# Attention probabilities transposed in 32x32 tiles by VectorE and regrouped by two transfers, in place of TensorE, for 16 of 24 heads

## The chip, the core and the metric

The kernel runs on one core of a Trainium2 chip. The metric is the device time of one execution, in microseconds (us). The kernel before took 937.93 us (median of 3 runs, 937.87 to 938.56). A separate, profiled execution gave the trace that is read here.

The core has engines that each work through their own list of instructions strictly in order: PE (TensorE, matrix products), DVE (VectorE), ACT (ScalarE), POOL (GpSimd), and SP, which in this kernel only issues transfers (DMAs). An instruction whose input is not ready makes everything behind it on that engine wait.

## What is computed

A decoder trunk of two layers on 256 tokens of width 1024, in float32. Each layer is a half-step SwiGLU FFN, a mixer, and a second half-step FFN. Both mixers hold softmax attention with heads of 64: layer 0 has 8 heads of masked attention (three dilation patterns, which one additive mask expresses) beside a gated MLP; layer 1 has 16 heads of causal attention, since with 256 tokens there is only the own block.

```
for layer in range(DEPTH):
    h = h + 0.5 * swiglu(rms_norm(h, ffn1_norm[layer]), ...)
    hn = rms_norm(h, mix_norm[layer])
    h = h + (ab_mixer(hn, ...) if layer % 2 == 0 else c_mixer(hn, ...))
    h = h + 0.5 * swiglu(rms_norm(h, ffn2_norm[layer]), ...)
return rms_norm(h, final_norm)
# attention of one head:  p = softmax(q k^T * scale + mask);  out = p v
```

## The kernel before

**Products in three parts.** Every float32 operand is split into a high part (rounded to fp32r, by ACT) and a low part (the rest, by DVE), and a product is three matmuls, high by high, high by low, low by high (`mm3`, L265). Of the weights, each chunk of 128x2048 is loaded by SP into one of 3 `raw` buffers (L139), split by ACT (`whi`, L172) and DVE (`wlo`, L173) into one of 4 buffer pairs, and used by PE. A chunk's load waits for the split that frees its `raw` buffer.

**The mixers.** `ab_mixer` (layer 0) and `c_mixer` (layer 1) run projections tile by tile, and a table of slots (`Slots`) says behind which tile a step of the attention is issued: one slot is one tile of 24 matmuls with 256 columns (or 12 with 512). The steps of a head are these.

- `put_q`, `put_k` turn a projected tile into the q and k of a pair of heads: for k DVE multiplies by the norm (`qk`, L659), ACT writes the high part (L683), POOL or DVE the low part (L685).
- `scores(h)`: four matmuls (L700, L701); DVE adds the mask and takes the maximum for each half (L704, two instructions with their reads `nm`); ACT takes the exponentials and their sums (L707); DVE the reciprocal `rl` (L710); POOL multiplies the probabilities `pr` by it, in two instructions (L714), for all but the last heads, where DVE does.
- `turn(h)`: PE transposes the head's 128x384 probabilities in three instructions (L723) into PSUM; ACT and DVE split them into `pth` and `ptl` (`split`, L271).
- `weighted(p)`: six matmuls multiply v by the probabilities of a pair of heads; ACT and DVE split the result into the tiles `mix` (L271).

In `ab_mixer`, DVE and ACT also prepare the gated part between these: `put_v` (`vtl`, L821), `keep_g` with the normalized `vn` (L853, by way of ACT's gelu and squares, DVE's `msg` and POOL's `rsg`), `put_u` (`uT`, L882), and `mixing(g)`, for which PE multiplies `vn` (L859) and DVE adds and multiplies (`tmp`, L864 and L865).

The order on each engine is made by the scheduler of the framework from the program's own order and what is ready. The last FFN already contains a transposition of the kind that the change adds: `turn_back` (L486) turns 128x128 in 32x32 tiles by DVE (L491), sends it to a scratch in memory (L494) and fetches it regrouped (L496).

## Time and profile before

| | us |
|---|---|
| median of 3 runs | 937.93 |
| the profiled execution, as timed | 937.01 |
| its span, first to last instruction | 935.3 |
| PE busy in the span | 927.7 |
| DVE busy | 612.1 |
| ACT busy | 499.2 |
| POOL busy | 83.0 |

The profile shows, for one execution, the busy time of each engine, the chain of work that ended last (followed back from the end, at each step to what released it), groups of instructions by line, and a timeline. In a group's row stand the line, the engine, the operation, written tile <- read tiles, shape and number, then busy us and the mean ns of one, then the engine's idle time before them and what ended it. In a timeline row stand the start in us, the duration, the engine and the instruction; the bracket at its end is the idle time before it and what ended that. SPq marks what SP issues.

### The profile page before, as it was taken

What the parts mean: (1) busy time and instruction counts of PE and PEld (TensorE: products, weight loads), DVE (VectorE), ACT (ScalarE), POOL (GpSimd) and SP (SyncE); (2) the same over time, 40 slices, a digit from 0 to 9 for tenths busy, and PEclk for the clock granted to TensorE, in tenths of its full rate; (3) what the DMA queues carried; (4) which work ended last, traced back from release to release, by engine and by line L of the source; (5) the groups of instructions that cost most, each with busy time, mean ns of one, the idle gap of its engine ahead of it and who ended that gap; (6) DMA issues with size and microseconds to landing.
All of it is one profiled execution on the core that took longest, in us unless ns stands there. A gap on an engine that the chain in (4) does not pass through costs nothing.

```text
span 935.3 us, 18101 instructions
## 1 busy us (share of the span) xinstructions
PE 927.7 (99%) x7655; PEld 907.4 (97%) x7655; DVE 612.1 (65%) x892; ACT 499.2 (53%) x782; POOL 83.0 (9%) x114
## 2 busy tenths in 40 slices
PE   9999999999999999999999999999999999999997
PEld 9999999999999999999999999999999999999886
DVE  7866556676888666555756665567787786656543
ACT  7744444468667454444454544456786665445431
POOL 0000000034210000000000000002574000000000
PEclk9999999999999999999999999999999999999999
DMA  8755554665336555555555555556543377555521
GB/s 320 281 212 181 189 194 162 223 222 180 136 136 226 188 211 188 183 175 206 204 184 200 204 180 170 203 184 220 177 139 136 137 243 269 186 188 210 190 90 46
DMA packets 28305, 176.99 MB, mean 189 GB/s; under 512 B 3264, under 2 KB 4672, under 8 KB 9152
## 3 DMA queue, kind: packets, MB, share of 16 engines
q1 hardware_dynamic: 26928, 173.65, 52.5%
q10 hardware_dynamic: 1296, 2.18, 0.7%
q8 instruction: 60, 0.98, 0.4%
q14 instruction: 21, 0.17, 0.0%
HBM read 173.72 MB, written 2.10 MB: 188 GB/s over the span
## 4 chain that ended last, share of the span: by engine, by line
PE 98%; issue 1%; DMA 0%; ACT 0%; SPq 0%; DVE 0%; POOLq 0%; POOL 0%
PE bank L266 30%; PE bank L267 30%; PE bank L268 30%; PE bank L567 2%; PE bank L571 2%; PE bank L568 2%; PE bank L723 1%; PE bank L700 1%; PE bank L701 1%; DMA x<-in_x 0%; PE bank L343 0%; PE bank L859 0%; PE bank L361 0%; PE bank L455 0%; PE bank L456 0%
## 5 line engine op out<-in xcount | busy, mean ns | idle before, releaser
L172 ACT ACTIVATE whi<-raw 128x1024 fp32r<-128x1024 f32 (+3 forms) x352 | 330.5, 985 | 350.1 <-issue 282.9
L173 DVE TENSOR_TENSOR wlo<-raw,whi 128x1024 fp32r<-128x1024 f32 (+3 forms) x352 | 389.6, 1141 | 126.7 <-ACT whi L172 125.8
L266 PE MATMUL bank<-xTh,whi 128*128 128x256 f32 x1616 | 447.9, 277 | 0.0
L267 PE MATMUL bank<-xTl,whi 128*128 128x256 f32 x1616 | 446.7, 276 | 0.0
L268 PE MATMUL bank<-xTh,wlo 128*128 128x256 f32 x1616 | 446.6, 276 | 0.0
L267 PEld LDWEIGHTS bank<-xTl,whi 128*128 128x128 f32 x1616 | 303.5, 188 | 0.2
L266 PEld LDWEIGHTS bank<-xTh,whi 128*128 128x128 f32 x1616 | 303.5, 188 | 0.0
L268 PEld LDWEIGHTS bank<-xTh,wlo 128*128 128x128 f32 x1616 | 303.5, 188 | 0.0
L267 PE MATMUL bank<-hTl,whi 128*128 128x256 f32 x528 | 145.8, 276 | 0.0
L266 PE MATMUL bank<-hTh,whi 128*128 128x256 f32 x528 | 145.8, 276 | 0.0
L268 PE MATMUL bank<-hTh,wlo 128*128 128x256 f32 x528 | 145.8, 276 | 0.0
L266 PEld LDWEIGHTS bank<-hTh,whi 128*128 128x128 f32 x528 | 99.1, 188 | 0.0
L268 PEld LDWEIGHTS bank<-hTh,wlo 128*128 128x128 f32 x528 | 99.1, 188 | 0.0
L267 PEld LDWEIGHTS bank<-hTl,whi 128*128 128x128 f32 x528 | 99.1, 188 | 0.0
L506 DVE TENSOR_TENSOR hm<-gs,bank 128x512 f32<-128x512 f32 x44 | 30.1, 687 | 77.7 <-PE bank L268 77.3
L503 DVE TENSOR_TENSOR gs<-bank,row 128x512 f32<-128x512 f32 x44 | 30.0, 689 | 47.8 <-PE bank L268 47.8
L266 PE MATMUL bank<-mixh,whi 128*128 128x256 f32 x128 | 35.3, 281 | 0.0
L267 PE MATMUL bank<-mixl,whi 128*128 128x256 f32 x128 | 35.1, 277 | 0.0
L268 PE MATMUL bank<-mixh,wlo 128*128 128x256 f32 x128 | 35.0, 277 | 0.0
L714 POOL TENSOR_SCALAR pr<-pr,rl 128x128 f32<-128x128 f32 (+1 forms) x36 | 30.8, 870 | 25.2 <-DVE rl L710 14.1
L653 POOL MEMSET ql<- 64x256 f32 x12 | 3.7, 307 | 328.7 <-ACT whi L172 170.3
L567 PE MATMUL bank<-whi,hTh 128*128 128x512 f32 x80 | 31.1, 389 | 0.0
(134 smaller groups left out, 877.4 us busy)
## 6 DMA issues: line engine op xcount, KB each, us to landing
raw<-in_weights SPq DMA_DIRECT2D x149, 1024.0 KB, 4.9
raw<-in_weights SPq DMA_DIRECT2D x12, 768.0 KB, 4.4
raw<-in_weights SPq DMA_DIRECT2D x6, 512.0 KB, 6.5
x<-in_x SPq DMA_DIRECT2D x4, 264.0 KB, 4.0
raw<-in_weights SPq DMA_DIRECT2D x4, 256.0 KB, 4.3
away<-xn SPq DMA_DIRECT2D x2, 512.0 KB, 5.5
xr<-away SPq DMA_DIRECT2D x8, 128.0 KB, 5.7
fg<-in_final_norm ACTq DMA_DIRECT2D x1, 512.0 KB, 3.7
```

What stands on the lines that cost most here:

```text
L172: nc.scalar.activation(hi, r, AF.Copy)
L173: nc.vector.tensor_sub(lo, r, hi.bitcast(F32))
L266: nc.tensor.matmul(p, sh, mh, start=start, stop=False)
L267: nc.tensor.matmul(p, sh, ml, start=False, stop=False)
L268: nc.tensor.matmul(p, sl, mh, start=False, stop=stop)
L503: nc.vector.tensor_mul(g, both(pg), twice(norm["row"]))
L506: nc.vector.tensor_mul(hm, g, both(pu))
L567: nc.tensor.matmul(banks[t, h], sh, w[0][kw][:, cs], start=k == 0, stop=False)
L568: nc.tensor.matmul(banks[t, h], sh, w[1][kw][:, cs], start=False, stop=False)
L571: nc.tensor.matmul(banks[t, h], sl, w[0][kw][:, cs], start=False, stop=k == FT - 1)
L700: nc.tensor.matmul(sc[:, b * S : (b + 1) * S], q[:, bs], k, start=True, stop=False)
L714: share = engine.tensor_scalar(pr[:, cs], pr[:, cs], rl[:, b : b + 1], None, op0=ALU.mult)
```

## The change

For the heads below `nheads - 4` (4 of 8 in layer 0, 12 of 16 in layer 1) the transposes by PE and the split out of PSUM are gone. In their place:

- Once POOL has scaled a head's `pr`, DVE transposes its 32x32 tiles into a tile `turned` that four heads share (L722 of the changed kernel, a `StreamTranspose` of 128x12x32). Four heads form a group.
- Behind the fourth head, `send` issues 12 transfers from SP's queue to a scratch in memory, each 32 partitions with 4x128 elements (runs of 512 bytes).
- Some slots later, `fetch` issues two transfers that read the scratch back, regrouped, one for each pair of heads, each 128 partitions with 12 runs of 64 elements (256 bytes).
- Some slots later again, `part` splits what was fetched: ACT copies (128x768) into `pth` and DVE subtracts into `ptl`, both placed behind the last split of weights (`issue_after`).

`weighted` for these heads stands 4 to 7 slots later than before, and in layer 1 the scores of heads 4 to 11 one or more slots earlier. The last four heads of each layer keep the transposes by PE. The buffers `pr` and `qk` become fewer, a gap tile becomes smaller, and the order of elements in `pth` and `ptl` changes, so that a product's moving operand is contiguous.

In the built program of the changed kernel 24 transposes are left on PE of 72; all other matmuls stay. DVE's list gets 16 `StreamTranspose` and loses 16 of the 128x384 subtractions for 8 of 128x768; on SP's queue the 12 transfers of a group, one or two loads of weights, and the two transfers of `fetch` follow each other.

```diff
@@ -34,7 +34,7 @@
 LINE, SHIFT = 64, 16
-EDGE, GAP = 56, 240
+EDGE, GAP = 56, 112

@@ -169,8 +169,7 @@
                 hi, lo = (t.rearrange("p (k c) -> p k c", k=reset) for t in (hi, lo))
-            nc.scalar.activation(hi, r, AF.Copy)
-            nc.vector.tensor_sub(lo, r, hi.bitcast(F32))
+            self.last = nc.scalar.activation(hi, r, AF.Copy), nc.vector.tensor_sub(lo, r, hi.bitcast(F32))

@@ -644,8 +643,9 @@

-        qs, ks, probs, pts = {}, {}, {}, {}
-        pairs, flying = (4, 5) if rows else (2, 4)
+        qs, ks, probs, pts, sent = {}, {}, {}, {}, {}
+        pairs = 4 if rows else 2
+        late = nheads - 4
         seconds = [mp.tile([128, 2 * S + LINE], F32R, name=f"ql{i}") for i in range(pairs)]
@@ -655,7 +655,7 @@
         def scaled(bk):
-            t = mp.tile([128, S], F32, name="qk", bufs=3)
+            t = mp.tile([128, S], F32, name="qk", bufs=2)
             nc.vector.tensor_mul(t, bk[:, :S], norm["row"])
@@ -692,7 +692,13 @@
             sc = bank()
-            pr = mp.tile([128, 384], F32, name="pr", bufs=flying)
+            if h % 4 == 0:
+                probs["turned"] = mp.tile([128, 3, 4, 4, 32], F32, name="turned")
+            turned = probs["turned"]
+            if h < late:
+                pr = mp.tile([128, 384], F32, name="pr", bufs=3)
+            else:
+                pr = turned.rearrange("p m j h r -> p (m j h r)")[:, h % 4 * 384 : (h % 4 + 1) * 384]
             nm = wk.tile([128, 2], F32, name="nm")
@@ -712,8 +718,41 @@
                 share = engine.tensor_scalar(pr[:, cs], pr[:, cs], rl[:, b : b + 1], None, op0=ALU.mult)
+            if h < late:
+                nc.vector.transpose(turned[:, :, :, h % 4].rearrange("p m j r -> p (m j) r"),
+                                    pr.rearrange("p (b c) -> p b c", c=32))
+                if h % 4 == 3:
+                    send(h // 4)
             probs[h] = pr
             return power, share
+
+        def send(g):
+
+            sent[g] = dram.tile([4, 32, 3, 4, 128], F32, name=f"sent{nheads}{g}")
+            for i in range(4):
+                for m in range(3):
+                    nc.sync.dma_start(sent[g][:, :, m, i].rearrange("j c f -> c j f"),
+                                      probs["turned"][i * 32 : (i + 1) * 32, m].rearrange("c j h r -> c j (h r)"))
+
+        def fetch(g):
+
+            src = sent.pop(g).rearrange("j c m i f -> (j c) (m i) f")
+            for q in range(2):
+                pts[2 * g + q] = parts = part_tiles()
+                nc.sync.dma_start(parts[1].bitcast(F32).rearrange("p b h r -> p b (h r)"),
+                                  src[:, :, q * 64 : (q + 1) * 64])
+
+        def part(g):
+
+            with tc.issue_after(st.last[0].ins), tc.issue_after(st.last[1].ins):
+                for q in range(2):
+                    hi, lo = pts[2 * g + q]
+                    nc.scalar.activation(hi, lo.bitcast(F32), AF.Copy)
+                    nc.vector.tensor_sub(lo, lo.bitcast(F32), hi.bitcast(F32))
+
+        def part_tiles():
+
+            return [mp.tile([128, 12, 2, 32], F32R, name=n, bufs=2) for n in ("pth", "ptl")]

@@ -722,21 +761,22 @@
             if j == 0:
-                pts[p] = [mp.tile([128, 2, 384], F32R, name=n, bufs=2) for n in ("pth", "ptl")]
-            return split(pts[p][0][:, j, :], pts[p][1][:, j, :], tp[:, :384])
+                pts[p] = part_tiles()
+            return split(*(t[:, :, j] for t in pts[p]), tp[:, :384].rearrange("p (b r) -> p b r", r=32))

         def weighted(p):
-            o = bank().rearrange("p (j c) -> p j c", j=2)
-            pth, ptl = pts.pop(p)
+            o = bank()
+            parts = [t.rearrange("p b h r -> p (b h r)") for t in pts.pop(p)]
             vs = slice(p * 128, (p + 1) * 128)
-            mm3(o, v[0][:, 0, vs], v[1][:, 0, vs], pth[:, :, :256], ptl[:, :, :256], True, False)
-            mm3(o[:, :, 128:], v[0][:, 1, vs], v[1][:, 1, vs], pth[:, :, 256:], ptl[:, :, 256:], False, True)
+            mm3(o, v[0][:, 0, vs], v[1][:, 0, vs], *(t[:, :512] for t in parts), True, False)
+            mm3(o[:, 256:], v[0][:, 1, vs], v[1][:, 1, vs], *(t[:, 512:] for t in parts), False, True)
             for j in range(2):
                 r = slice(j * 64, j * 64 + 64)
-                done = split(mix[0][r, p], mix[1][r, p], o[r, j, :].rearrange("p (t c) -> p t c", t=NT))
+                done = split(*(m[r, p].rearrange("p t (i r) -> p (t i) r", r=32) for m in mix),
+                             o[r].rearrange("p (b h r) -> p b h r", h=2, r=32)[:, :, j])
             return done

-        return put_q, put_k, scores, turn, weighted
+        return put_q, put_k, scores, fetch, part, turn, weighted

@@ -827,7 +867,7 @@
             uT = mp.tile([128, 4, S], F32, name="uT")
-            put_q, put_k, scores, turn, weighted = make_attention(mp, slice(0, 384), 8, v, mix)
+            put_q, put_k, scores, fetch, part, turn, weighted = make_attention(mp, slice(0, 384), 8, v, mix)

@@ -872,10 +912,12 @@
             slots.at((21,), lambda _: st.release(tc, scores(7), True))
-            slots.at((10, 10, 12, 12, 22), turn)
+            slots.at((13,), fetch)
+            slots.at((17,), part)
+            slots.at((22,), lambda _: turn(4))
             slots.at((22,), lambda _: st.release(tc, turn(5), True))
             slots.at((23, 23), lambda i: turn(6 + i))
-            slots.at((13, 14, 24), weighted)
+            slots.at((18, 19, 24), weighted)
             slots.at((25,), lambda _: st.release(tc, weighted(3)))
@@ -896,12 +938,14 @@
             v = v_tiles(mp, D)
-            put_q, put_k, scores, turn, weighted = make_attention(mp, slice(384, 768), 16, v, mix, True)
+            put_q, put_k, scores, fetch, part, turn, weighted = make_attention(mp, slice(384, 768), 16, v, mix, True)

             slots = Slots()
-            slots.at((5, 6, 7, 8, 12, 13, 14, 15, 16, 17, 18, 19, 24, 24, 25, 25), scores)
-            slots.at((9, 9, 11, 11, 16, 16, 18, 18, 20, 20, 22, 22, 26, 26, 27, 27), turn)
-            slots.at((11, 13, 18, 20, 22, 24, 28, 29), weighted)
+            slots.at((5, 6, 7, 8, 11, 12, 13, 14, 15, 16, 17, 18, 24, 24, 25, 25), scores)
+            slots.at((14, 20, 25), part)
+            slots.at((15, 16, 21, 22, 26, 27, 28, 29), weighted)
+            slots.at((12, 17, 23), fetch)
+            slots.at((26, 26, 27, 27), lambda i: turn(12 + i))
             step = slots.step
```

## Prediction

> **What bounds the kernel now.** I read the share of each engine first, then the chain that ended last, the idle time of PE by what ended it, and then timelines around the attention.
>
> ```profile
> PE 927.7 (99%) x7655; PEld 907.4 (97%) x7655; DVE 612.1 (65%) x892; ACT 499.2 (53%) x782; POOL 83.0 (9%) x114
> PE 98%; issue 1%; DMA 0%; ACT 0%; SPq 0%; DVE 0%; POOLq 0%; POOL 0%
> ```
>
> ```profile
> PE bank L442 <- DVE warm L435: 1.1, 1, 1.1
> ```
>
> The chain is PE from end to end, and the only wait of PE that the trace lists is the one of 1.1 us at the start. So time comes off only if PE gets less to do, and every late operand is added in full. The mean shares of DVE and ACT hide how full they are beside the attention of layer 1:
>
> ```profile
> 660.00:670.00 10.00, 10.00 (x80) 9.60 (x79) 6.91 (x20) 7.42 (x19) 6.25 (x10) 1.00 0.59 202
> 680.00:690.00 10.00, 10.00 (x87) 9.87 (x86) 8.99 (x26) 7.47 (x22) 7.11 (x9) 1.00 0.49 154
> ```
>
> In this view of windows the columns behind PE and PEld are DVE, ACT and POOL: from 680 to 690 us DVE works 8.99 of 10 us, with PE at 10.00. A wait put on DVE there has hardly any idle time to go into.
>
> **What is removed.** Each row below is the transposes of two heads.
>
> ```profile
> 219.84 0.66 PE bank L723 x6
> ...
> 715.50 0.66 PE bank L723 x6
> ```
>
> They are the first and the last of the eight groups that go (16 heads); four more stay. Gain if PE never waits: 8 x 0.66 = **5.3 us**. The products with the probabilities keep their matmuls, so nothing else comes off PE.
>
> [...]
>
> **What is added on DVE.** The operation itself has a neighbour in the last FFN, and the slope with size is seen where one line runs with two widths:
>
> ```profile
> L491 DVE STREAM_TRANSPOSE xn<-x 128x128 f32<-128x128 f32 x16 | 3.6, 278 | 0.0
> L704 DVE CUSTOM_DVE_ANT_0 pr<-bank,mask 128x256 f32<-128x256 f32 x8 | 3.3, 419 | 0.0
> L704 DVE CUSTOM_DVE_ANT_0 pr<-bank,mask 128x128 f32<-128x128 f32 x8 | 2.3, 285 | 0.0
> L173 DVE TENSOR_TENSOR wlo<-raw,whi 128x768 fp32r<-128x768 f32 x26 | 23.8, 954 | 26.1 <-ACT whi L172 25.8
> L173 DVE TENSOR_TENSOR wlo<-raw,whi 128x1024 fp32r<-128x1024 f32 x272 | 324.3, 1225 | 91.5 <-ACT whi L172 91.1
> L172 ACT ACTIVATE whi<-raw 128x768 fp32r<-128x768 f32 x26 | 20.7, 839 | 39.6 <-issue 39.6
> ```
>
> A transposition of 128x384 is at least 0.28 us and at most 3 x 0.278 = 0.83. With 134 ns more for each 128 columns it is 278 + 2 x 134 = 546 ns; I take 0.55. Of the split, one instruction of 128x768 takes 0.95 on DVE and 0.84 on ACT, where a pair of 128x384 took 1.0 and 0.86 (rows below), so the work there stays as it is.
>
> The duration matters less than the wait in front of it. In the built program each transposition stands right behind its head's reciprocal `rl`, or a few instructions later, and waits for POOL's share of that head. These rows show how long that is:
>
> ```profile
> 659.56 0.16 DVE L710 RECIPROCAL rl<-l 128x2 f32<-128x2 f32 x1
> 660.29 0.74 DVE L821 SCALAR_TENSOR_TENSOR vtl<-bank,rstd,vth 128x512 fp32r<-128x512 f32 x1
> 662.83 0.35 DVE L704 CUSTOM_DVE_ANT_0 pr<-bank,mask,score 128x128 f32<-128x128 f32 x1 [1.57 <-PE bank L701]
> 668.59 0.17 DVE L710 RECIPROCAL rl<-l 128x2 f32<-128x2 f32 x1 [0.40 <-ACT pr L707]
> 669.74 1.31 DVE L173 TENSOR_TENSOR wlo<-raw,whi 128x1024 fp32r<-128x1024 f32 x1 [0.98 <-ACT whi L172]
> 671.42 1.00 DVE L271 TENSOR_TENSOR ptl<-bank,pth 128x384 fp32r<-128x384 f32 x2
> 674.17 0.42 DVE L659 TENSOR_TENSOR qk<-bank,row 128x256 f32<-128x256 f32 x1
> ```
>
> ```profile
> 659.88 3.00 POOL L714 TENSOR_SCALAR pr<-pr,rl 128x128 f32<-128x128 f32 x4 [2.58 <-DVE rl L710]
> 666.18 1.50 POOL L714 TENSOR_SCALAR pr<-pr,rl 128x128 f32<-128x128 f32 x2 [3.30 <-DVE rl L710]
> 675.13 1.54 POOL L685 TENSOR_TENSOR k<-qk,k 64x256 fp32r<-64x256 f32 x2 [2.46 <-ACT k L683]
> ```
>
> POOL starts 659.88 - 659.56 = 0.32 behind `rl` and takes 1.50 for a head's two instructions. The transposition can start 1.8 us after `rl`, and until then DVE does only what the list puts between the two: one `vtl` (0.7), one mask pair (0.285 + 0.419 = 0.7), or nothing. Everything behind it on DVE waits too: masks of the next heads, splits of weights, `qk`.
>
> **What is moved.** In layer 1 the scores of head 4 stand one slot earlier on PE, and the transposes and the product that stood before them are gone or later. PE therefore asks sooner for what DVE now brings later.
>
> ```profile
> 665.38 0.28 PE L700 MATMUL bank<-k,q 128*128 128x256 f32 x1
> ...
> 679.11 0.28 PE L700 MATMUL bank<-k,q 128*128 128x256 f32 x1
> ...
> 736.33 0.40 PE L266 MATMUL bank<-pth,vth 128*128 128x512 f32 x1
> ...
> 737.38 0.28 PE L266 MATMUL bank<-mixh,whi 128*128 128x256 f32 x1
> ```
>
> The first two rows are the scores of heads 3 and 4, 13.73 us apart: four tiles, the four score matmuls (0.46), two transposition groups (2 x 0.66) and one product of a pair (737.38 - 736.33 = 1.05). A tile is thus (13.73 - 0.46 - 1.32 - 1.05)/4 = 2.72. In the changed list three tiles and the scores are left, 8.6: PE asks **5.1 us** sooner.
>
> *Scores of head 4.* They wait for k, that is DVE's `qk`, ACT's high part, POOL's low part. In the changed list the four transpositions before `qk` stand behind 0.7, 0, 0.7 and 0 of other work, so DVE waits 1.1 + 1.7 + 1.0 + 1.7, about 5.4, and works 4 x 0.55 = 2.2. Off go the subtractions of heads 0 and 1 (1.0), and the old idle times 1.57 + 0.40 + 0.98 = 3.0 soak up as much. DVE is late by 5.4 + 2.2 - 1.0 - 3.0 = 3.6. The low part of k was ready at 675.13 + 1.54/2 = 675.9, a margin of 3.2 to 679.11. Stall: 5.1 + 3.6 - 3.2 = **5.5**.
>
> *From there to the product of heads 0 and 1.* DVE must do five mask pairs (3.5), four `rl` (0.7), the splits of two and a half chunks (five halves of 1.2, 6.1), six 64- or 128-row pieces of q and k (0.42 each, 2.5), four transpositions (2.2) and the first `ptl` (0.95): 15.9. Three of the waits add 3.3 (1.8 less 0.55, 0.7 and 0.7 of work between). PE has four tiles (10.9), five heads' scores (2.3) and five matmuls of 0.23 before the one that reads `ptl`: 14.3. Stall: 19.2 - 14.3, about **4.8**. Groups 1 and 2 follow the same list, but their waits find the slack that these two stalls have made: 0.
>
> *Layer 0, `mixing(0)`.*
>
> ```profile
> 214.23 1.22 DVE L173 TENSOR_TENSOR wlo<-raw,whi 128x1024 fp32r<-128x1024 f32 x1 [0.51 <-ACT whi L172]
> 217.50 0.17 DVE L710 RECIPROCAL rl<-l 128x2 f32<-128x2 f32 x1 [0.84 <-ACT pr L707]
> ...
> 229.71 1.01 DVE L271 TENSOR_TENSOR ptl<-bank,pth 128x384 fp32r<-128x384 f32 x2
> 233.21 1.14 DVE L853 SCALAR_TENSOR_TENSOR vn<-gv,rsg,vgain 128x128 f32<-128x128 f32 x4 [1.12 <-POOL rsg L274]
> ```
>
> ```profile
> 236.81 0.61 PE L859 MATMUL bank<-wsT,vn 128*128 128x128 f32 x4
> ```
>
> Its second matmul reads the `vn` of the second token tile, whose first quarter was ready at 233.21 + 0.35, a margin of 3.3. Two transposition groups and two products no longer stand before it, so PE asks 1.32 + 2.10 = 3.4 sooner. DVE waits 1.0 + 1.0 + 1.5 + 1.7 = 5.2 for POOL and transposes for 2.2, saves two pairs of `ptl` (2.0) and the idle 0.51 + 0.84: late by 4.05. Stall: 3.4 + 4.05 - 3.3, about **4.1**. From there to the product of heads 0 and 1 DVE's list is 10.3 and PE's 9.1, worked out in the same way: **1.2**.
>
> **The transfers** I cost at nothing, because DVE's list covers them:
>
> ```profile
> 769.58 1.64 SPq L496 DMA_DIRECT2D xr<-away  x3
> ```
>
> ```profile
> DMA to landing us min/median/max: 3.6/5.7/7.3
> ```
>
> One issue is 1.64/3 = 0.55. `rl` of head 3 stood at 668.59; three waits and transpositions before it (1.1 + 1.7 + 1.0 + 1.65), less 1.57 + 0.40 of idle time, put it at 672.1, and 1.8 + 0.55 later, at 674.5, the fourth transposition is done. Twelve issues (6.6), a landing of 3.6, two more issues (1.1) and a landing of 5.7 to 7.3 end by 693.1. DVE starts on head 4's mask at about 679.5 (674.0 + 5.5) and comes to `ptl`, 18.2 of work and waits later, at 697.7. Cover: some 5 us, less ACT's 0.84. SP's queue holds weight loads behind them, which land 9 to 14 us before they are split and have two more chunks behind that; a delay of about 10 us fits.
>
> **The sum**, on the profiled execution: 937.0 - 5.3 + 5.5 + 4.8 + 4.1 + 1.2 = 947.3. The median lies 0.9 over that execution, so **948.2**. Twelve transpositions lie in these stalls: at 0.28 each the sum falls by 3.2 (945), at 0.83 it grows by 3.4 (952). POOL's shares, 1.5 here, took up to 2.4 where DVE worked beside them, which adds up to 3. Own range 942 to 954.
>
> **Rivals.**
> *PE stays dense.* The scheduler's list is strict, but if DVE's waits fall into idle time that I counted as needed, only the 5.3 is seen: 932.6. For it: DVE has 35% idle over the span. Against: both windows above.
> *DVE is on time, the transfers decide.* Then the last transposition of a group is done at 668.59 + 1.8 + 0.55 = 671, the fetch lands 17.0 to 18.6 later, and with ACT's 0.84 and DVE's 0.95 `ptl` is ready at 689.8 to 691.4. A dense PE asks for it at 674.0 + 14.3 = 688.3: 1.5 to 3.1 short, and three such groups make 932.6 + 7 = 939.6. Against it: it needs the first rival's condition.
> *Stalls cost more than their length.* After its first idle time PE ran slow:
>
> ```profile
> 1.10 4.57 PE L442 MATMUL bank<-warm 128*128 128x128 f32 x22 [1.10 <-DVE warm L435]
> ```
>
> That is 208 ns each where the transposes take 110, 2.1 us lost. If each of the three stalls above 4 us brings that back, 948.2 + 6.4 = 954.6. [...]
>
> **How the numbers follow.** Chances: forecast 0.54, dense PE 0.16, transfers 0.13, slow clock 0.17. What a measurement of this kernel can tell from no change is about 0.2%, 1.9 us. Below 936.05 lies the dense case: 0.16. The transfers' case reaches into the band with 0.03. The rest, 0.81, is slower. The dense case is left out of the range, the others are taken in: 936 to 957.
>
> **What would show it.** In the changed profile PE should wait about 5 us for POOL's k before the scores of head 4 of layer 1, 4 to 5 us for DVE's `ptl` before the first product with a fetched tile, and 4 us for `vn` in layer 0; DVE's transposes should each have 1 to 1.7 us of idle time ended by POOL's `pr`. PE waiting for a DMA there, or a PE without waits, would prove me wrong; so would transposes far from 0.55 us.

## The result, and the profile after

| | before | changed |
|---|---|---|
| median of 4 runs, us | 937.90 (937.12 to 938.56) | 963.34 (961.34 to 966.95) |
| the profiled execution, as timed | 937.01 | 961.34 |
| its span | 935.3 | 959.6 |

The changed kernel takes 1.0276 times as long, with a 95% interval of 1.0239 to 1.0312. It is slower by 25.4 us, where 10.3 had been forecast; 963.3 lies outside the range of 936 to 957. The profiled execution is longer by 24.3 us, and all but some 0.5 of them lie in two short stretches, the attention of either layer. One run each of late_turn and of use_only below was some 2% slower than the others and is left out of their medians; that of use_only is the profiled one, so only the places of its waits are read.

The page of the changed kernel first.

```profile
PE 932.8 (97%) x7607; PEld 909.9 (95%) x7607; DVE 619.7 (65%) x900; ACT 498.3 (52%) x774; POOL 78.3 (8%) x114
...
PE 86%; DVE 5%; ACT 4%; POOL 2%; issue 2%; DMA 0%; POOLq 0%; DVEq 0%; ACTq 0%
```

PE has 48 matmuls fewer (7607 for 7655), and yet is counted busy 5 us longer; and the chain that ended last now passes through DVE, ACT and POOL, where it was PE alone. Both have to be explained. The waits of PE, by what ended them (us in total, how often, the longest):

```profile
PE bank L706 <- POOL k L685: 6.9, 2, 5.4
PE bank L265 <- ACT pth L750: 5.7, 2, 3.0
PE bank L899 <- DVE vn L893: 4.2, 1, 4.2
PE bank L266 <- DVE ptl L751: 2.0, 3, 1.2
...
PE bank L762 <- POOL turned L720: 0.6, 1, 0.6
```

Before, only a wait of 1.1 us at the start was in this list; it is still there. The five shown sum to 19.4 us. Where they lie, PE's timeline tells; the bracket is the idle time before the instruction and what ended it.

```profile
238.46 0.49 PE L899 MATMUL bank<-wsT,vn 128*128 128x128 f32 x2 [4.24 <-DVE vn L893]
...
685.33 0.58 PE L706 MATMUL bank<-k,q 128*128 128x256 f32 x1 [5.45 <-POOL k L685]
...
702.34 0.39 PE L706 MATMUL bank<-k,q 128*128 128x256 f32 x1 [1.49 <-POOL k L685]
706.11 0.79 PE L265 MATMUL bank<-pth,vth 128*128 128x512 f32 x1 [3.03 <-ACT pth L750]
730.63 0.50 PE L266 MATMUL bank<-ptl,vth 128*128 128x512 f32 x1 [1.21 <-DVE ptl L751]
...
753.44 0.50 PE L265 MATMUL bank<-pth,vth 128*128 128x512 f32 x1 [2.71 <-ACT pth L750]
```

The first is `mixing(0)` in layer 0, the second the scores of head 4 in layer 1. The next two are the scores of head 8 and, right behind them, the product of heads 0 and 1; the last two belong to the products of groups 1 and 2.

Some of the matmuls behind these waits run at half speed. In the view of windows the column to look at is the granted clock, the third figure from the end:

```profile
238.40:243.00 4.60, 4.54 (x25) 4.54 (x26) 3.90 (x10) 2.30 (x4) 0.00 (x0) 0.63 1.12 305
685.30:689.80 4.50, 4.47 (x21) 4.47 (x22) 3.21 (x7) 3.35 (x8) 2.75 (x4) 0.50 0.71 220
706.00:710.00 4.00, 3.89 (x11) 2.97 (x12) 4.00 (x5) 2.23 (x5) 2.94 (x2) 0.50 0.45 119
753.40:756.00 2.60, 2.13 (x9) 1.68 (x10) 2.44 (x3) 0.73 (x1) 0.00 (x0) 0.77 0.64 189
756.00:760.00 4.00, 4.00 (x23) 3.56 (x22) 2.40 (x6) 2.56 (x7) 0.00 (x0) 0.72 0.55 229
```

From 685.30 to 689.80 PE is busy without a break, but does 21 matmuls of 256 columns, 213 ns each, where it does about 40 at 113. So a busy PE can also be a slow PE: this is why its busy time grew. Window by window, length times (1 - clock) is 1.7 + 2.25 + 2.0 + 0.6 + 1.1, about 7.7 us lost.

So the 24.3 us are made up: 5.3 less for the transposes; stalls of about 21.0, taken from the starts of successive matmuls (the waits of 19.4 above are each some 0.2 longer when measured in this way); 7.7 for the slow clock. The sum is 23.4; half a microsecond more is lost before the first layer's attention, and the rest is not assigned.

What DVE and ACT do ahead of these waits. Two groups of instructions, with busy time, mean ns, and the idle time in front of them:

```profile
L722 DVE STREAM_TRANSPOSE turned<-pr 128x384 f32<-128x384 f32 x16 | 9.0, 573 | 15.2 <-POOL pr L720 14.9 <-DVE rl L716 0.3
...
L750 ACT ACTIVATE pth<-ptl 128x768 fp32r<-128x768 f32 x8 | 6.6, 832 | 0.0
```

The 16 transpositions were preceded by 15.2 us of idle time, nearly all of it ended by POOL (12 waits). The second row answers for the transfers: ACT had no idle time (0.0) before any of the eight copies of fetched tiles, so it never stood waiting for a fetch: each had landed at least 6.6 us before its copy began. DVE's timeline ahead of k of head 4 in layer 1:

```profile
665.29 0.16 DVE L716 RECIPROCAL rl<-l 128x2 f32<-128x2 f32 x1
...
667.17 0.58 DVE L722 STREAM_TRANSPOSE turned<-pr 128x384 f32<-128x384 f32 x1 [1.06 <-POOL pr L720]
...
670.08 0.58 DVE L722 STREAM_TRANSPOSE turned<-pr 128x384 f32<-128x384 f32 x1 [1.63 <-POOL pr L720]
...
675.41 0.58 DVE L722 STREAM_TRANSPOSE turned<-pr 128x384 f32<-128x384 f32 x1 [0.98 <-POOL pr L720]
...
679.84 0.58 DVE L722 STREAM_TRANSPOSE turned<-pr 128x384 f32<-128x384 f32 x1 [1.70 <-POOL pr L720]
...
683.60 0.76 DVE L659 TENSOR_TENSOR qk<-bank,row 128x256 f32<-128x256 f32 x2
```

The four waits sum to 5.4 us and each transposition takes 0.57, as in the forecast's step; `qk`, at 674.17 before, is now at 683.60. Layer 1 as a whole stands 5.7 us later here (this `rl`, at 665.29, was at 659.56), so `qk` is late by 3.7, where the forecast had 3.6. And ACT ahead of the first product with a fetched tile:

```profile
703.02 1.04 ACT L172 ACTIVATE whi<-raw 128x1024 fp32r<-128x1024 f32 x1
703.97 0.84 ACT L683 ACTIVATE k<-qk 64x256 fp32r<-64x256 f32 x2
704.83 0.40 ACT L713 ACTIVATE pr<-pr,nm 128x128 f32<-128x128 f32 x1
...
705.23 0.83 ACT L750 ACTIVATE pth<-ptl 128x768 fp32r<-128x768 f32 x1
```

The copy `pth`, for which PE stands still from 703.1, is the last in a row of work without a gap. Directly ahead of it stand the exponentials of head 8 (704.83), whose scores PE worked out at 702.34, just before it asked for `pth`. Whether this order costs a stall even when DVE is on time, late_turn and first_copy test.

### The profile page after: what moved, and what is told of

It is laid out like the page before. It is cut to its first block, busy times and chain, and to the rows that moved or that the text cites. A ratio compares the mean times of both kernels' runs of the same rounds, so it can differ in the third digit from the quotient of the medians.

```text
span 959.6 us, 18082 instructions
## 1 busy us (share of the span) xinstructions
PE 932.8 (97%) x7607; PEld 909.9 (95%) x7607; DVE 619.7 (65%) x900; ACT 498.3 (52%) x774; POOL 78.3 (8%) x114
## 4 chain that ended last, share of the span: by engine, by line
PE 86%; DVE 5%; ACT 4%; POOL 2%; issue 2%; DMA 0%; POOLq 0%; DVEq 0%; ACTq 0%
PE bank L266 26%; PE bank L265 26%; PE bank L267 26%; DVE wlo L172 3%; PE bank L567 2%; PE bank L570 2%; PE bank L566 2%; POOL pr L720 2%; ACT whi L172 1%; ACT pr L713 1%; DVE ql L673 1%; PE bank L441 1%; DMA raw<-in_weights 0%; ACT q L672 0%; ACT k L683 0%
## 5 line engine op out<-in xcount | busy, mean ns | idle before, releaser
L567 PE MATMUL bank<-wlo,hTh 128*128 128x512 f32 x80 | 31.1, 389 | 0.0
L270 DVE TENSOR_TENSOR hTl<-hm,hTh 128x512 fp32r<-128x512 f32 x44 | 30.2, 686 | 1.4 <-ACT hTh L270 1.4
```

The costliest lines, as they stand in the source:

```text
L270: return nc.scalar.activation(hi, src, AF.Copy), nc.vector.tensor_sub(lo, src, hi.bitcast(F32))
L567: nc.tensor.matmul(banks[t, h], sh, w[1][kw][:, cs], start=False, stop=False)
```

## The experiments

W is the theory that DVE stands still behind `rl` until POOL's share is done, and that PE waits for what stands behind. D puts it down to the transpositions' own work, X to the transfers. All times are medians, against 937.0 to 937.9 for the kernel before, run beside them; PE's stalls are read as above.

| kernel | us | ratio to before, 95% |
|---|---|---|
| changed kernel | 963.3 | 1.0239 to 1.0312 |
| no_turn: DVE's transpositions left out | 940.7 | 1.0014 to 1.0039 |
| dve_scale: DVE scales, not POOL | 953.8 | 1.0133 to 1.0192 |
| late_turn: transposition behind the next `rl` | 952.9 | 1.0116 to 1.0182 |
| part_first: last group's copies ahead of splits | 957.9 | 1.0162 to 1.0231 |
| use_only: fetched tiles used later | 966.1 | 1.0285 to 1.0336 |
| first_copy: ACT's order at group 0 | 964.2 | 1.0270 to 1.0306 |
| later_use: late_turn with use_only | 952.3 | 1.0128 to 1.0247 |
| later_first: that with part_first | 949.0 | 1.0107 to 1.0137 |
| later_all: that with layer 0 later | 953.4 | 1.0157 to 1.0217 |
| act_order: late_turn, copies ahead in all groups | 948.0 | 1.0084 to 1.0118 |
| k_later: that with two scores later | 948.7 | 1.0102 to 1.0132 |
| layer1_only: that with layer 0 as before | 946.5 | 1.0078 to 1.0133 |

**no_turn**

```diff
             if h < late:
-                nc.vector.transpose(turned[:, :, :, h % 4].rearrange("p m j r -> p (m j) r"),
-                                    pr.rearrange("p (b c) -> p b c", c=32))
+                if h % 4 == 0:
+                    nc.vector.memset(turned, 0.0)
                 if h % 4 == 3:
+                    nc.vector.tensor_copy(turned[:, 0, 0, 3, :2], rl)
                     send(h // 4)
```

> The 16 transpositions by DVE are left out: the tile that is sent is set to zero once for each group, and a write of two columns behind the fourth head's rl keeps the time from which the transfers may start; everything else stays. W and D: no stall before vn and k of head 4 but up to 1 us, the first fetched products up to 1.5 us, and only the stall of 2.9 us before the last group's product stays, since it is made by ACT's order: 937 to 942. X: the transfers start at most 3 us sooner, so stalls of about 3 us before each group's first fetched product stay: 947 or more.

940.7: the transpositions with their waits are worth 22.7 us together. Even without them the kernel is 3 us slower than before, since the many short waits of PE outweigh the 5.3 us of transposes. Among them are these, none longer than 1.2:

```profile
PE bank L706 <- POOL k L685: 1.9, 2, 1.2
PE bank L900 <- DVE vn L894: 1.2, 1, 1.2
...
PE bank L265 <- ACT pth L751: 0.4, 1, 0.4
```

X falls: with the same 48 + 8 transfers PE waits 0.4 us for a fetched tile. But the run cannot tell W from D, and it changes one thing more: in its built list ACT's copy of group 0 stands ahead of head 7's exponentials, so this kernel lacks that stall for a second reason.

**late_turn**: the same work, without the wait.

```diff
-            nc.vector.reciprocal(rl, l)
+            recip = nc.vector.reciprocal(rl, l)
...
+            if waiting:
+                regroup(recip)
             if h < late:
-                nc.vector.transpose(turned[:, :, :, h % 4].rearrange("p m j r -> p (m j) r"),
-                                    pr.rearrange("p (b c) -> p b c", c=32))
-                if h % 4 == 3:
-                    send(h // 4)
+                waiting.append((h, turned, pr))
...
+        def regroup(behind):
+
+            h, turned, pr = waiting.pop(0)
+            with tc.issue_after(behind.ins):
+                nc.vector.transpose(turned[:, :, :, h % 4].rearrange("p m j r -> p (m j) r"),
+                                    pr.rearrange("p (b c) -> p b c", c=32))
+            if h % 4 == 3:
+                send(h // 4, turned)
...
+            slots.at((11,), lambda _: regroup(st.last[1]))
...
+            slots.at((10, 15, 20), lambda _: regroup(st.last[1]))
```

The last two lines are for the fourth head of a group, in layer 0 and in layer 1; `st.last[1]` is DVE's latest split of weights.

> Each transposition is put behind the next head's rl, the fourth of a group behind a later instruction of DVE, so that POOL has finished before DVE comes to it. The same work on every engine, but no wait. W: DVE's idle time ended by POOL's pr falls from 14.9 us to under 4; the stalls at vn and at k of head 4 fall from 4.4 and 5.6 to under 1.5 each, and the slow matmuls behind them are gone. The transfers of group 0 of layer 1 start some 3 us later against a PE that is 5 us ahead, so up to 5 us of stall can appear before the first fetched product, then ended by the fetch: 945 to 954. D: 963 as before, since no work is taken away. X: slower than 963, since the transfers start later.

952.9. DVE's waits for POOL in front of transpositions fell from 14.9 us to 2.2, and with them PE's waits at `vn` and k; the list of PE's waits, and ACT ahead of the first product:

```profile
PE bank L265 <- ACT pth L758: 7.1, 2, 4.0
...
PE bank L706 <- POOL k L685: 1.7, 2, 1.0
PE bank L907 <- DVE vn L901: 1.2, 1, 1.2
```

```profile
693.56 0.40 ACT L713 ACTIVATE pr<-pr,nm 128x128 f32<-128x128 f32 x1
...
694.46 1.04 ACT L172 ACTIVATE whi<-raw 128x1024 fp32r<-128x1024 f32 x1
695.40 1.56 ACT L758 ACTIVATE pth<-ptl 128x768 fp32r<-128x768 f32 x2
```

D falls for these stalls: no work was taken away, and 4.24 became 1.2, and 5.45 at most 1.0. The stall before the first product did not become shorter: 3.03 before, 4.0 now. I had allowed up to 5 us there, ended by the fetch; it is ended by ACT, whose copy again stands behind head 8's exponentials and a split, with no wait for a transfer.

**dve_scale** takes the same wait away at the price of work.

```diff
-                engine = nc.gpsimd if h < nheads - (4 if rows else 2) else nc.vector
+                engine = nc.gpsimd if late <= h < nheads - (4 if rows else 2) else nc.vector
```

> DVE multiplies the probabilities of the 16 changed heads by rl itself (two instructions, about 0.55 us for a head) in place of POOL, so a transposition no longer waits for another engine, but DVE has more work. Theory W (DVE stands still behind rl until POOL's share is done, and PE waits for what stands behind it): the waits of 1.0 to 1.7 us are gone for 0.5 us of work, PE's stalls fall from 4.4 to about 1 (layer 0, vn), from 5.6 to about 2.5 (k of head 4), from 1.7 + 3.2 to about 3.5 (first fetched product); two stalls above 4 us are gone and with them the slow matmuls behind them (about 4 us). In all about 948 to 952. Theory D (the work of the transpositions themselves makes DVE late): DVE's list is 0.5 us longer for each head, 963 or above. Theory X (the two transfers come late): unchanged, 961 to 967.

953.8, 1.8 above the range given for W and 9 below what D asks. The waits at `vn` and k:

```profile
235.98 0.49 PE L899 MATMUL bank<-wsT,vn 128*128 128x128 f32 x2 [1.85 <-DVE vn L893]
...
679.42 0.50 PE L706 MATMUL bank<-k,q 128*128 128x256 f32 x1 [1.94 <-POOL k L685]
```

Of 4.24 and 5.45 there are 1.85 and 1.94 left, where about 1 and 2.5 were expected; the third, expected at 3.5, is 4.48 and ended by ACT, as in late_turn. The wait of 1.94 was followed by half clock (0.50 from 679.54 to 682.95), though it is short.

**part_first** changes the last group of layer 1 alone.

```diff
-            slots.at((14, 20, 25), part)
+            slots.at((24,), lambda _: st.hold())
+            slots.at((14, 20), part)
+            slots.at((25,), lambda _: st.release(tc, part(2)))
```

`part` returns its last copy and subtraction here, and the held split of weights is issued behind them.

> Only the last group of layer 1 is changed: ACT's and DVE's copies of the fetched tiles stand ahead of the splits of the last weight chunks, not behind them. If ACT's order makes the stall of 2.9 us before that product (its copy stands behind two splits which wait for a buffer that PE frees with the matmuls just before), the stall falls to 1 us or less and the slow matmuls behind it (about 1.7 us) are gone: 958 to 960. If the fetch itself comes late there, the stall and the time stay: 961 to 967.

957.9, as expected. The wait of 2.71 for `pth` at group 2 is gone; what is left there is one of 1.51 for ACT's `mixh`, the split of that product. So the 2.71 came from ACT's order. In the changed kernel the copy, at 752.56, stood behind two splits that waited for a buffer of PE:

```profile
750.65 2.00 ACT L172 ACTIVATE whi<-raw 128x1024 fp32r<-128x1024 f32 x2 [1.09 <-PE bank L266]
```

**use_only, first_copy, later_use**: three ways to the stall before the first product. The first diff is use_only's, and later_use's on top of late_turn.

```diff
-            slots.at((14, 20, 25), part)
-            slots.at((15, 16, 21, 22, 26, 27, 28, 29), weighted)
-            slots.at((12, 17, 23), fetch)
+            slots.at((16, 21, 25), part)
+            slots.at((17, 18, 22, 23, 26, 27, 28, 29), weighted)
+            slots.at((12, 18, 23), fetch)
```

> The changed kernel with only the use of the fetched tiles in layer 1 moved: part of group 0 two slots later and of group 1 one slot later, the products of heads 0 to 3 two slots later, those of heads 4 to 7 one, the fetch of group 1 one. DVE waits for POOL as before. Theory W with ACT's order (ACT's copy of the first fetched tile stands behind head 8's exponentials, whose scores PE works out just before the product): the stalls of 4.4 us (vn) and 5.6 us (k of head 4) stay with the slow matmuls behind them; the stall of 3.2 us before the first product and the slow matmuls behind it (in all about 5.5 us) go, since two more tiles lie between: 956 to 959. If DVE's list alone were too long in this stretch, the 5 us would come back at the next products: 961 to 966.

> The same move of the uses on top of the kernel whose transpositions stand behind the next head's rl (953.2 us). There PE stands still for 4.1 + 0.4 + 1.8 + 0.4 us around the first product, with 2.4 us lost by slow matmuls. If ACT's order and the early use make these: they go, 943 to 946. If the transfers make them (the fetch lands too late): PE is asked two tiles later, 5.4 us, so most goes as well, but a wait of ACT for the fetch is then seen in the trace. If the work of DVE makes them: 950 or more.

Neither gain came: 966.1 and 952.3 are the times of the alternatives in which DVE has too much to do (961 to 966, and 950 or more). The stall in question did go in both (0.3 us is left at the first product), but another came at group 1. In later_use, PE, and ACT ahead of that wait:

```profile
719.56 0.50 PE L265 MATMUL bank<-pth,vth 128*128 128x512 f32 x1 [3.52 <-ACT pth L758]
```

```profile
715.38 2.00 ACT L172 ACTIVATE whi<-raw 128x1024 fp32r<-128x1024 f32 x2
717.79 0.85 ACT L683 ACTIVATE k<-qk 64x256 fp32r<-64x256 f32 x2 [0.41 <-DVE qk L659]
718.67 1.58 ACT L758 ACTIVATE pth<-ptl 128x768 fp32r<-128x768 f32 x2
```

A wait of 1.83 for `ptl` follows. The transfers are not the reason: issued at 705.08 and 705.66, as soon as the products of group 0 had freed the buffers, they landed at 712.4 and 713.9, and ACT began its copy at 718.67. It stands behind two splits and the newest k, which waited for DVE. PE, held up less at group 0, comes sooner than these two lists. Which of the two holds it back more was not separated.

first_copy puts, on ACT, head 8's exponentials and the last k behind the copy, in the changed kernel:

```diff
+                with tc.issue_after(probs["behind"].ins) if rows and h in (8,) else ExitStack():
                     power = nc.scalar.activation(pr[:, cs], pr[:, cs], AF.Exp, bias=nm[:, b : b + 1], scale=-1.0,
                                                  accum_out=l[:, b : b + 1])
...
+                with tc.issue_after(probs["behind"].ins) if rows and p in (5,) else ExitStack():
                     nc.scalar.activation(k[r, :], t[r, :], AF.Copy)
...
-            slots.at((14, 20, 25), part)
+            slots.at((13,), lambda _: st.hold())
+            slots.at((14,), lambda _: st.release(tc, part(0)))
+            slots.at((20, 25), lambda i: part(1 + i))
```

> The changed kernel with only the order on ACT turned round at group 0 of layer 1: ACT's copies of the first fetched tiles stand ahead of the next weight splits, of the last k before the product and of head 8's exponentials (the splits are held back for it, on DVE too, so that DVE's list before ptl is about 3 us shorter). The transpositions, their waits for POOL and all slots stay. If ACT's order made the stall of 3.2 + 0.4 us before the first product, it falls to 1 us or less, the 1.7 us before it (k behind POOL) may stay, and the slow matmuls behind it (1.6 us) go: 957 to 960. If DVE's waits make it, the same 3 us are then waited for ptl: 961 to 966.

964.2, so the gain expected from ACT's order did not come; the time is that of the second alternative. PE around the product shows what happened:

```profile
703.48 0.50 PE L265 MATMUL bank<-pth,vth 128*128 128x512 f32 x1 [0.57 <-ACT pth L752]
707.09 0.80 PE L266 MATMUL bank<-ptl,vth 128*128 128x512 f32 x1 [1.67 <-DVE ptl L753]
...
732.54 0.79 PE L266 MATMUL bank<-ptl,vth 128*128 128x512 f32 x1 [2.97 <-DVE ptl L753]
```

The wait for `pth` fell from 3.03 to 0.57, and a wait of 1.67 for `ptl` came, a few matmuls later; at group 1 the wait for `ptl` grew from 1.21 to 2.97, more than was won here. DVE's list was shorter here, so on the changed kernel's own list, where DVE came to `ptl` at 706.80, it would have been later still. So there were two limits at that place: DVE with its waits for POOL, and ACT's order. Taking one away leaves the other (late_turn and dve_scale the one way, first_copy the other).

**later_first, later_all, act_order, k_later, layer1_only** try to bring it together. later_first is later_use with part_first; later_all then moves layer 0 by one slot; act_order is late_turn with the copies of all three groups of layer 1 ahead of the held splits, and group 0 one slot later; k_later has scores in slots 12, 12, 14, 14 in place of 11 to 14; layer1_only gives layer 0 back to PE. The diff is act_order's on top of late_turn; beside it, the exponentials of heads 9 and 10 stand behind the copy in the way of first_copy.

```diff
-            slots.at((14, 20, 25), part)
-            slots.at((15, 16, 21, 22, 26, 27, 28, 29), weighted)
+            slots.at((14,), lambda _: st.hold())
+            slots.at((19,), lambda _: st.hold())
+            slots.at((24,), lambda _: st.hold())
+            slots.at((15,), lambda _: st.release(tc, part(0)))
+            slots.at((20,), lambda _: st.release(tc, part(1)))
+            slots.at((25,), lambda _: st.release(tc, part(2)))
+            slots.at((16, 17, 21, 22, 26, 27, 28, 29), weighted)
```

> Further, the copies of the last group's fetched tiles stand ahead of the splits of the last weight chunks. The stalls of 3.3 + 0.4 + 1.2 us there and 1.9 us of slow matmuls fall to about 1.5 in all: 938 to 942. If the fetch is late there, the time stays at that of the kernel before it, 943 to 946.

> Further, in layer 0 the fourth transposition stands behind vn of the first token tile, and mixing, fetch, part and the products of heads 0 to 3 stand one slot later. The stalls at vn (1.3 us), before ptl (0.8) and 0.4 go: 936 to 940, about the kernel before. If no stall is left, PE does 5.3 us less than before: 932.6. If layer 0's slack is used up, the stall comes back before ptl and the time stays at 938 to 942.

> From the kernel whose transpositions stand behind the next head's rl (953.2 us): in layer 1 the splits of weights are held back behind the copies of the fetched tiles in all three groups, the exponentials of heads 9 and 10 stand behind the first copies, and group 0's copies and products stand one slot later; groups 1 and 2 keep their slots. If the place of ACT's copy in ACT's list (behind splits that wait for PE, and behind exponentials whose scores PE works out just before the product) makes the stalls at the fetched products, those of layer 1 (4.1 + 0.4 + 1.8 + 0.4, then 3.3 + 0.4 + 1.2, and 3.8 of slow matmuls) fall to 3 in all or less: 940 to 944. If the fetch is late, ACT is seen to wait for it and a stall of 2 us or more stays at each product: 946 or more.

> Further, the scores of heads 4 and 6 stand one slot later (so behind the tile that hides k's way through DVE, ACT and POOL). The stalls of 1.2 us at k of heads 4 and 6 go, if early asking makes them: 2 us less than act_order. If DVE is simply full there, the same time comes back at the first product: no change against act_order.

> As k_later, but the four heads of layer 0 are transposed by PE again, at the slots of before, and without transfers. Layer 0 then costs 1.3 us of PE and has no stall; in the others it has about 3 us of stalls. So 1.5 us less than k_later, and if layer 1 has under 2.5 us of stalls left, this is the first kernel to be faster than before: 936 to 940.

They came out at 949.0, 953.4, 948.0, 948.7 and 946.5, none below the kernel before. later_first and later_all lie above all that was expected of them; act_order has the time of its second alternative, without the late fetch that was to make it; k_later is no faster than act_order, its second alternative; layer1_only gains 2.2 us on k_later, where 1.5 were expected, but stays above 940. part_first's step was worth 3.4 us here (952.3 to 949.0), against 5.4 in the changed kernel. later_all removed the stall at `vn` and got one of 5.51 us before the first product of layer 0 for it. k_later won nothing: one wait at k went, and that for `ptl` at group 0 grew (0.61 to 1.45). In act_order 0.8 us of stall is left at group 0, and group 1 holds most of the rest; ACT ahead of its copy:

```profile
713.68 0.40 ACT L714 ACTIVATE pr<-pr,nm 128x128 f32<-128x128 f32 x1 [0.18 <-DVE nm L710]
...
714.69 0.38 ACT L672 ACTIVATE q<-bank 64x256 fp32r<-64x256 f32 x1
715.09 1.58 ACT L759 ACTIVATE pth<-ptl 128x768 fp32r<-128x768 f32 x2
```

The splits are behind it now, but head 11's exponentials and the newest q are still ahead. That group's transfers, issued at 703.33 and 703.96, had landed by 710.0, three microseconds before PE stopped, so they leave room for a copy ahead of those too; this was not tried.

**pauses, short_pauses** put artificial idle time into PE of the kernel before: PE transposes, DVE works through a chain on the result, PE transposes that, and the next tile stands behind. They took 972.8 and 953.6 us, one run each.

```diff
+    def pause(n):
+        p = bank()
+        nc.tensor.transpose(p[:, :128], ident, ident)
+        t = wk.tile([128, 128], F32, name="pause", bufs=1)
+        nc.vector.tensor_copy(t, p[:, :128])
+        for _ in range(n):
+            nc.vector.tensor_scalar(t, t, 1.0, None, op0=ALU.mult)
+        gate.append(nc.tensor.transpose(bank()[:, :128], t, ident))
```

> The kernel before with four artificial pauses of PE in layer 1, each made by a chain of DVE instructions between two transposes by PE (4, 8, 13 and 19 instructions of 128x128 behind a copy, so of some 2 to 6 us, the first longer where other work falls in between). It measures what a pause costs beyond its length. If there is a threshold at about 4 us, the short ones are followed by matmuls at full speed (113 ns for 256 columns), and those above by about 20 matmuls at 213 ns, some 2 us. If every pause costs the same, slow matmuls follow each. If a pause costs its length only, none.

> The kernel before with four shorter artificial pauses of PE in layer 1 (chains of 0, 1, 3 and 6 DVE instructions behind a copy). The pauses of 4.6 to 8.2 us cost 1.7 to 2.7 us more than their length. If there is a threshold between 2 and 4 us, pauses of 1 to 2 us are followed by no slow matmul and the sum of all excess but the pauses stays under 0.5 us; if each pause costs the same, 1.7 us or more follow each.

The three longer pauses of the short kernel (the first was of 0.38 us):

```profile
682.81 0.33 PE L771 MATMUL bank<-ident,pause 128*128 128x128 f32 x1 [2.11 <-DVE pause L770]
698.26 0.30 PE L771 MATMUL bank<-ident,pause 128*128 128x128 f32 x1 [2.74 <-DVE pause L770]
729.04 0.48 PE L771 MATMUL bank<-ident,pause 128*128 128x128 f32 x1 [4.66 <-DVE pause L770]
```

The pause of 2.11 us was followed by half clock for 3.41 us, which costs 1.7 us more than its length; that of 4.66 by half clock until 734.73, 5.69 x 0.50 = 2.8 us; that of 2.74 by none. In the kernel with longer pauses those of 4.73 and 4.48 us were followed by clocks of 0.50 (673.70 to 678.00) and 0.61 (691.70 to 696.00), and the two longer ones, of up to 8.2, by slow matmuls as well: the four cost 1.7 to 2.7 us each more than their length. So every pause above 4 us was paid a second time, and between 2 and 3 us it came out either way.

The granted clock shows where the two differ. In the trace of the changed kernel it is 1.00 or 0.50, and the slow stretches in the attention begin at 239.40, 683.13, 703.61 and 754.81, that is 130, 6 and 15 times 3.413 us apart. Laid out at this spacing from the slow stretch that begins at 683.52 in the short kernel, the 2.11 us lie within one window, while the 2.74 are cut in two:

```profile
680.11:683.52 3.41, 1.30 (x12) 1.08 (x11) 2.92 (x6) 1.16 (x4) 0.91 (x2) 1.00 0.25 58
683.52:686.93 3.41, 3.41 (x18) 3.41 (x18) 0.93 (x5) 0.99 (x4) 1.40 (x2) 0.50 0.59 250
693.76:697.17 3.41, 1.75 (x16) 1.53 (x14) 2.52 (x8) 3.31 (x10) 3.15 (x5) 1.00 0.67 276
697.17:700.58 3.41, 2.32 (x13) 2.06 (x14) 2.81 (x8) 1.77 (x4) 3.25 (x3) 1.00 0.16 19
```

The first figure behind the length is PE's busy time: PE stood idle for 2.11 us of the first window, and the next has half clock; it stood idle for 1.66 and 1.09 of the last two, and the clock stayed. In the changed kernel the windows just ahead of its slow stretches, from 235.98, 679.72, 700.20 and 751.40, hold 2.48, 3.25, 2.01 and 2.25 us of idle PE; of the others before 950 us the two with the most idle PE hold 1.75 (from 232.57) and 1.21 (from 727.50), and the clock stayed at 1.00 behind them. In later_use a window with 1.35 us was followed by half clock, so that no limit is shown.

## Why the prediction was wrong

It had the sign and the first two stalls right, and the size wrong by 15 us. Two steps failed, the last two of this list: stalls put at 0 that measured 5.3 us, and a price of a stall that left out 7.7.

- *The gain, 5.3.* PE has 48 transposes fewer, at 0.66 us for six (110 ns each) in the profile of before. It stands.
- *The transposition, 0.55.* 573 ns were measured. The waits in front: four of together 5.4 in layer 1 (5.4 forecast).
- *Scores of head 4, 5.5.* 5.45, ended by POOL's k, as said, and its terms hold: DVE was late by 3.7 for 3.6. late_turn, which keeps the work and removes the wait, brings it to 1.0 at most: the wait was the cause.
- *`mixing(0)`, 4.1.* 4.24, ended by DVE's `vn`; with late_turn 1.2. The 1.2 for the first `ptl` of layer 0 did not show; 0.6 was waited at another place of layer 0, for POOL's `turned`, so that the sum of these stalls fits partly by luck.
- *The product of heads 0 and 1, 4.8.* 1.49 for k and 3.03 for `pth` make 4.5. The size was right and the reasoning half of it: I followed DVE's list only. ACT's list holds a second limit, the copy behind head 8's exponentials. first_copy and late_turn show both. Each takes one away and keeps a stall.
- *The transfers, 0.* Hidden, as said: ACT had no idle time before any copy of a fetched tile, and with the transfers alone (no_turn) PE waits 0.4 us at most.
- *Groups 1 and 2, "0".* This step failed. It let the waits of those groups vanish in slack that the first stalls had made, without following a list. (The products of the changed heads stand 2 to 5 slots later than before, not 4 to 7 as said above, so there was less room than it seemed.) PE waited 1.2 us there for `ptl` and 2.71 for `pth`, with smaller gaps and measured by starts some 5.3 in all. The smaller is the forecast's own wait: `ptl` stands behind a transposition that waited 1.64 for POOL, and in late_turn, without that wait, 0.1 is left. The larger has nothing to do with slack: `part` is put behind the last split of weights, this split waits for a buffer which PE frees with the matmuls just before the product, and ACT then needs two microseconds for it and the one behind it. part_first shows it.
- *A stall costs its length.* This was the forecast's choice, and the larger mistake: 7.7 us. The case with slow matmuls was written down as a rival, priced at 6.4 for three stalls, and given 0.17. The profile of before had the row that speaks for it, 208 ns for the first matmuls, and nothing against it; with three stalls above 4 us in the forecast it belonged into the sum. The pauses show that the idle time itself brings it (clock 0.50 behind 4.73 us). The rival was right there, and its size nearly (6.4 for 7.7).

With those two terms the working would have read 947.3 + 5.3 + 7.7 = 960.3 on the profiled execution, for 961.3.

## What to carry to other kernels

Where PE never waits, work taken off PE is paid back by the first operand that comes late (here 5.3 us came off, and about 21.0 of stalls came in); so follow the list of each engine on the new path up to the operand, ACT's as well as DVE's, and look for an instruction that stands behind work which itself needs PE's newest result. A wait put into an engine's list counts for everything behind it: here a transposition of 0.57 us stood still for up to 1.7 for POOL, and issuing it one head later gave back 10 of 25 us. Price the slow matmuls behind a stall too: here those of 4.24 and 5.45 us and every pause above 4 were followed by them, 1.7 to 2.8 us on top; of the shorter ones, those of 1.94 (dve_scale) and 2.11 us were, that of 2.74 was not.

## What the runs showed of the hardware

Behind the stall of 5.45 us, matmuls of 256 columns took 213 ns in place of 113. The clock was at 0.50 for 3.41 us or 6.83 at a time in the attention of the changed kernel, and for 10.0 of the 12 us from 692 to 704 in late_turn; part of it can lie within the stall (2.2 us of it before the wait of 5.45 ended). What lies behind cost 1.7 to 2.8 us in the changed kernel and in the two with pauses. It came behind the stalls of 4.24 and 5.45 us and each pause above 4, behind one of 2.11 and dve_scale's stall of 1.94, and not behind one of 2.74. The transposition of 128x384 in float32 in 32x32 tiles took 573 ns on DVE, 191 ns for 128 columns, less than the 278 of a separate one of 128x128. A transfer of 12 runs of 256 bytes in each of 128 partitions landed after 6.1 us (median of 8), and the 48 transfers of 64 KB to memory after 1.8.
